# Low parts of every second output projection tile built by an accumulating DMA, and the last head's products put into score banks

## The chip, the cores and the metric

The kernel runs on one core of a Trainium2 chip (trn2). The metric is the device time in microseconds (us) of one execution. The core's engines run side by side, each through its own list of instructions in order: TensorE (PE, matrix products, with its weight loads as a row of their own, PEld), VectorE (DVE), ScalarE (ACT) and GpSimd (POOL). SyncE (SP) issues nearly all transfers, which sixteen DMA engines carry out.

## The reference

Two layers (`DEPTH = 2`) of a hybrid decoder trunk over 512 tokens, with 16 learned meta tokens put in front (`T = 528` columns in all), width 1024, all in float32. Each layer runs a causal pooling mixer and a latent attention with 8 heads beside each other on the same normalised input:

```python
h = RMSNorm(x)
[u_pool | z_pool | c_q | c_kv | k_rope | z_mla | g_pool | g_mla] = h @ W_in
y_pool = W_pool_up( PoolMix(u_pool) * silu(z_pool) )
y_mla  = W_mla_up( MLA(c_q, c_kv, k_rope) * silu(z_mla) )
x = x + W_out( sigmoid(g_pool) * y_pool + sigmoid(g_mla) * y_mla )
```

`MLA` normalises the latent query and key/value rows, expands them to 8 heads of 64 + 32 elements (the 32 with a rotary position), normalises queries and keys per head, and takes a causal softmax over the keys. The meta positions are dropped from the output.

## The kernel before

**Precision by splitting.** A float32 product is made of three products of a faster type (`fp32r`). A weight chunk `raw` of 128 rows by up to 512 columns is fetched by an SP DMA (`raw<-win`, `raw<-wout`, ...). `wload` then makes the high part `whi` with a Copy on ACT (L179) and the low part `wlo = raw - whi` with a subtraction on DVE (L180). Activations are split in the same way (L275, L276). `mm3` multiplies `whi·xh`, `whi·xl` and `wlo·xh` (L184, L185, L186) into the same PSUM accumulator.

**Staging.** `raw`, `whi` and `wlo` have three buffers each. Tiles marked `spare` (the odd `mu` tiles, L1005) take the pool `th`/`tl` instead. `stream()` is one generator over all weight tiles of both layers, in the order of `plan`: it loads up to four chunks ahead, and a tile of width 1024 (`D`) has two chunks of 512 columns. So a chunk of 512 columns feeds four 128x128 weight blocks, and each block is used in three products over every column segment: two segments of 264 columns in layer 0, one of 512 columns in layer 1 (the last tile of layer 1: two of 256).

**Order.** `Layer.go` writes the rest by hand: norms, pooling, attention heads and meta tokens are emitted at points of the stream, with `fill_now(ns)`, `fill(...)`, `up(name)` and `after(ns, fn)` letting so much of the stream pass between them. The order of each engine's instructions is then fixed once, when the kernel is built, by a scheduler that models time (`schedule_with_timeline_sim=True`). At run time each engine goes through its list and waits on semaphores.

**The places that the change touches.**

- `norm_sums` (L370): the row sums for the first norm, the products of ones with squares (L389), a short Newton chain on DVE for the inverse roots (`newton`), a write to DRAM (`ndr<-ny`, L420), and a read back spread over all partitions (`rinv<-ndr`, L426). In layer 0, `tables()` makes the rotary sine and cosine (DVE L293 to L303, ACT L300 and L301) between the write and the read.
- `pv` (L823): the product of a head's probabilities with its values. The probabilities are transposed into an `mm` bank, split into `th`, `tl` on ACT and DVE, and multiplied into the bank `o` (L845, L846). Odd heads also put four products for the meta tokens into a bank `tr` (L849 to L852), which ACT copies out (`racc`, L854).
- PSUM: `mmt()` gives one of four `mm` banks, `sct()` one of three score banks `S`, which are free once the last head's scores have been used; `o` is one bank.
- `meta_queries` (L877): in layer 0, the attention of the 16 meta queries from all heads' scores, called when the last head's first products and 2600 ns of stream have been emitted. Its second half comes `2 * LAG` later, and `meta_out` (L907) fills the 16 meta columns of `ogs`, which the first `mu` tile reads.
- `mu{m}` (L1004) and `o{m}` (L1008): eight tiles each per layer, at its end. `o{m}` is the output projection: 16 chunks of `wout` per layer, evicted by `ev_o` with a DVE instruction (L942).

Of the kernel before, what the change touches and what calls it, by code (L numbers as in the profile page):

```python
# [18 lines left out]
P = 128  # L19
# [52 lines left out]
def trunk(ctx, tc, xT, xrow, mrow, pos, win, wkr, wqb, wkb, wvb, wgr, wpu, wmu, wout, gains, const, yT):  # L72
# [17 lines left out]
    def slot(tag, dt=F32, bufs=1, w=W):  # L90
        return sl.tile([P, w], dt, tag=tag, name=nm(tag), bufs=bufs)
# [69 lines left out]
    class Gemm:  # L161
        def __init__(self, name, src, width, evac=None, xs=None, segs=None, body=None, gain=None):
            self.name, self.src, self.width, self.alloc = name, src, width, mmt
            self.evac, self.xs, self.segs, self.body, self.gain = evac, xs, segs, body, gain
            self.spare = False

    loads = [0]

    def wload(src, n, gain, spare):
        raw = early.pop(0) if early else fetch(src, n, rawt(), sp)  # L170
        loads[0] += 1
        pool, th, tl, nb = (tp, "th", "tl", 2) if loads[0] <= 2 or spare else (wp, "whi", "wlo", 3)
        if gain is not None:
            v = raw[:, :n].rearrange("p (k m) -> p k m", k=8)
            gp.tensor_mul(v, v, gain.unsqueeze(2).to_broadcast([P, 8, n // 8]))
            return raw, None
        hi = pool.tile([P, W if pool is tp else 512], F32R, tag=th, name=nm("whi"), bufs=nb)
        lo = pool.tile([P, W if pool is tp else 512], F32R, tag=tl, name=nm("wlo"), bufs=nb)
        act.activation(hi[:, :n], raw[:, :n], AF.Copy)  # L179
        dve.tensor_sub(lo[:, :n], raw[:, :n], hi[:, :n].bitcast(F32))  # L180
        return hi, lo

    def mm3(out, wh, wl, xh, xl, start, stop):
# [8 lines left out]
    def stream():  # L192
        flat = [(g_, c) for g_ in plan for c in range(0, g_.width, 512)]
        flat[1], flat[2] = flat[2], flat[1]

        def load(i):
            g_, c = flat[i]
            n = min(512, g_.width - c)
            return wload(g_.src[:, c:c + n], n, g_.gain, g_.spare)

        ahead = []
        for i in range(4):
            ahead.append(load(i))
            yield 0.0
        for i, (g_, c) in enumerate(flat):
            w = ahead.pop(0)
            if i >= 3 and i + 1 < len(flat):
                ahead.append(load(i + 1))
            final = c + 512 >= g_.width
            if g_.body is not None:  # L210
                yield from g_.body(c // 512, w)
            else:
                xs = g_.xs()
                K = len(xs)
                if c == 0:
                    g_.pss = [g_.alloc() for _ in g_.segs]
                k0 = c // P
                for ps, (a, b) in zip(g_.pss, g_.segs):
                    n = b - a
                    for k in range(k0, min(K, k0 + 4)):  # L220
                        o = (k - k0) * P
                        mm3(ps[:, :n], w[0][:, o:o + P], w[1][:, o:o + P],
                            xs[k][0][:, a:b], xs[k][1][:, a:b], k == 0, k == K - 1)
                        if k < K - 1 and (k - k0) % 2 == 1:
                            yield 6 * (n / 2.4)
                    if final:
                        g_.evac(ps[:, :n], a, b)
                        if b == g_.segs[-1][1]:
                            done.add(g_.name)
                        yield 6 * (n / 2.4)  # L230
            if final:
                done.add(g_.name)
# [80 lines left out]
    class Layer:  # L313
# [56 lines left out]
        def norm_sums(self):  # L370
            if self.l:
                fill_now(2600)
            else:
                rows = self.row_sums()
                for _ in range(8):
                    step()
                while (0, "ckv1") not in done:
                    next(rows)
                for _ in range(4):
                    next(rows)  # L380
            px, pc = mmt() if self.l else None, mmt()
            xs = self.xsq[::4] if self.l else []
            runs = [(px, t, m, m < 2, m >= len(xs) - 2) for m, t in enumerate(xs)]
            runs += [(pc, t, m, True, True) for m, t in enumerate(self.csq)]
            for k in range(0, len(runs), 2):
                for s, (a, b) in enumerate(FULL):
                    for ps, t, m, start, stop in runs[k:k + 2]:
                        g = 64 * s + 32 * (m % 2)
                        mm = pe.matmul(ps[g:g + 32, :HALF], ones[:, 0:32], t[:, a:b], start=start, stop=stop,  # L389
                                       tile_position=(0, g))  # L390
                        if t is not self.csq[1]:
                            behind(mm, self.csq_last)
            sums = tmp()
            for s, (a, b) in enumerate(FULL):
                if self.l:
                    act.activation(sums[0:64, a:b], px[64 * s:64 * s + 64, :HALF], AF.Copy)
                dve.tensor_copy(sums[64:128, a:b], pc[64 * s:64 * s + 64, :HALF])
            raw, norms = nsr[self.l], ndr[self.l]
            if self.l:
                sp.dma_start(raw, sums[0:97:32, 0:T])  # L400
            else:
                sp.dma_start(raw[2:4], sums[64:97:32, 0:T])
                for _ in rows:
                    pass
            C = T // 16
            parts = lambda d: d.rearrange("i (s c) -> s i c", c=C)
            fill_now(2600)
            nq = sm.tile([16, 4, C], F32, tag="nq", name=nm("nq"))
            na, nt, ny = (sm.tile([16, n, C], F32, tag=t, name=nm(t)) for t, n in (("na2", 2), ("nt2", 2), ("ny2", 3)))
            sp.dma_start(nq, parts(raw))  # L410
            dve.tensor_scalar(na[:, 0, :], nq[:, 0, :], 1.0 / D, EPS, op0=ALU.mult, op1=ALU.add)
            dve.scalar_tensor_tensor(out=na[:, 0, :], in0=nq[:, 1, :], scalar=1.0 / D, in1=na[:, 0, :],
                                     op0=ALU.mult, op1=ALU.add)
            dve.tensor_scalar(na[:, 1, :], na[:, 0, :], EPS, None, op0=ALU.mult)
            dve.tensor_scalar(ny[:, 2, :], na[:, 1, :], EPS, None, op0=ALU.mult)
            for m in range(2):
                dve.scalar_tensor_tensor(out=na[:, 1, :], in0=nq[:, 2 + m, :], scalar=1.0 / 256,
                                         in1=na[:, 1, :], op0=ALU.mult, op1=ALU.add)
            newton(ny[:, 0:2, :], na, nt)
            sp.dma_start(parts(norms), ny)  # L420
            self.inv, self.cinv = slot("rinv"), slot("q1")
            if self.l == 0:
                tables()
            fill_now(RET)
            for i, d in enumerate((self.inv, self.cinv)):
                behind(sp.dma_start(d[:, 0:T], norms[i:i + 1, :].partition_broadcast(P)), newest[0])  # L426
            self.st = [sct(), sct()]
# [395 lines left out]
        def pv(self, prev, js):  # L823
# [2 lines left out]
            h, pt, pm = prev  # L826
            p, odd = h // 2, h % 2
            if js[0] == 0:
                self.o = pp.tile([P, 512], F32, tag="o", name=nm("o"), bufs=1)
            ops = self.o  # L830
            if odd == 1 and js[0] == 0:
                self.pmr = sm.tile([P, 4, 3, 32], F32R, tag="pmr", name=nm("pmr"))
# [13 lines left out]
                pe.matmul(out, vt[:, j, h, :], tl[:, :n], start=False, stop=j == 3)  # L846
            if js[-1] != 3:
                if odd == 1:
                    tr = mmt()  # L849
                    for i in range(4):  # L850
                        pe.matmul(tr[0:96, P * i:P * (i + 1)], self.pmr[:, i].rearrange("p a b -> p (a b)"), identr,
                                  start=True, stop=True)  # L852
                    self.mt = slot("racc", F32R)
                    act.activation(self.mt[0:96, 0:512], tr[0:96, :], AF.Copy)  # L854
                return
# [97 lines left out]
        def register(self, nxt):  # L953
# [52 lines left out]
            for m in range(8):  # L1006
                add(f"mu{m}", wmu[l, m], 512, evac=self.ev_mu(m), xs=lambda: self.ogs, segs=XS)
                plan[-1].spare = m % 2 == 1  # L1008
            mg = lambda: self.mg
            for m in range(8):  # L1010
                add(f"o{m}", wout[l, m], D, evac=self.ev_o(m, nxt), xs=mg,
                    segs=[(NM, NM + SEQ // 2), (NM + SEQ // 2, T)] if self.last and m == 7 else XS)

        def gap(self):
            fill(FILL[self.l], (self.l, RESERVE[self.l]))

        def go(self, nxt):
# [44 lines left out]
                self.gap()  # L1062
            fill_now(1300)
            self.pv(prev, (0, 1))
            fill_now(2600)
            if not self.last:
                self.meta_queries()
            self.pv(prev, (2, 3))
            up("gm7")
            flush()  # L1070
# [85 lines left out]
```

## Time and profile before

| | |
|---|---|
| median of 3 runs | 784.38 us (784.22 to 784.66) |
| profiled execution | 784.25 us |
| its span in the profile | 782.5 us |
| granted TensorE clock | 1.00 in all slices |
| share of the span busy | PE 99%, DVE 69%, ACT 53%, POOL 26% |
| weight chunks split on DVE (L180) | 251 |
| DMA queue that SP issues to | 82.86 of 84.04 MB |

Some 1.8 us of the profiled execution lie outside the span. An instruction row of the timeline gives its start, its length, the engine, the line, the operation, output and inputs, the shape, a count, and in brackets the idle time before it that something ended. A row of the waits gives the waiting group, the releaser, the total, the count and the longest. The two output projections of this execution lie at about 340 to 402 us (layer 0) and 728 to 780 us (layer 1).

### The profile page before, as it was taken

To read this page: it belongs to the slowest core of one execution; us is meant where nothing else is said; L and a number is where in the kernel's file an instruction comes from. 1 tells how busy PE (TensorE), PEld (TensorE's weight loads), DVE (VectorE), ACT (ScalarE), POOL (GpSimd) and SP (SyncE) were. 2 spreads that over 40 slices of the span, in tenths; PEclk is the share of its full clock that TensorE was granted. 3 is DMA by queue.
4 is the path that set the end of the run, shared out by engine and by line. 5 is a ranking of instruction groups with operands and counts; after the bars stand their busy time and mean duration, and the time that the engine had idled before them with its cause. 6 is when DMAs were issued, how large, how long until landed. Compare 5 with 4: busy or idle time off the path is not lost.

```text
span 782.5 us, 14500 instructions
## 1 busy us (share of the span) xinstructions
PE 776.2 (99%) x5235; PEld 705.7 (90%) x5235; DVE 538.0 (69%) x1163; ACT 411.5 (53%) x938; POOL 206.8 (26%) x265
## 2 busy tenths in 40 slices
PE   9999999999999999999999999999999999999998
PEld 9999899999999999999998898887788888887887
DVE  6588787357779977675365587774477888665932
ACT  6755656545656565533354356455446666554421
POOL 1035504012343242052120335130132333410500
PEclk9999999999999999999999999999999999999999
DMA  8533233333323212324643323324242332222372
GB/s 297 153 104 95 77 124 104 108 96 102 92 74 92 79 63 74 95 81 143 182 137 97 103 82 96 125 88 142 72 124 89 95 89 80 66 78 68 101 231 99
DMA packets 54931, 84.04 MB, mean 107 GB/s; under 512 B 10006, under 2 KB 18582, under 8 KB 54860
## 3 DMA queue, kind: packets, MB, share of 16 engines
q1 hardware_dynamic: 54716, 82.86, 34.8%
q8 instruction: 41, 0.67, 0.4%
q14 instruction: 30, 0.25, 0.1%
q10 hardware_dynamic: 144, 0.26, 0.1%
HBM read 76.68 MB, written 4.29 MB: 103 GB/s over the span
## 4 chain that ended last, share of the span: by engine, by line
PE 94%; DVE 3%; DMA 1%; ACT 1%; issue 1%; POOL 0%; SPq 0%; ACTq 0%; DVEq 0%; POOLq 0%
PE mm L184 28%; PE mm L185 27%; PE mm L186 27%; PE mm L840 2%; PE S L184 2%; PE S L185 1%; PE S L186 1%; PE o L846 1%; PE o L845 1%; PE S L495 1%; DMA rinv<-ndr 1%; PE mm L454 0%; DVE wlo L180 0%; DMA xb<-xT 0%; DMA raw<-wmu 0%
## 5 line engine op out<-in xcount | busy, mean ns | idle before, releaser
L184 PE MATMUL mm<-hh,whi 128*128 128x264 f32 (+2 forms) x1096 | 346.3, 318 | 0.4 <-DVE u L538 0.2
L185 PE MATMUL mm<-hl,whi 128*128 128x264 f32 (+2 forms) x1096 | 343.6, 315 | 0.0
L186 PE MATMUL mm<-hh,wlo 128*128 128x264 f32 (+2 forms) x1096 | 342.6, 315 | 0.0
L180 DVE TENSOR_TENSOR wlo<-raw,whi 128x512 fp32r<-128x512 f32 (+2 forms) x251 | 188.9, 756 | 109.4 <-ACT whi L179 105.6
L179 ACT ACTIVATE whi<-raw 128x512 fp32r<-128x512 f32 (+2 forms) x251 | 150.3, 602 | 178.3 <-PE mm L185 130.0
L184 PEld LDWEIGHTS mm<-hh,whi 128*128 128x128 f32 x1096 | 205.7, 188 | 14.1 <-issue 1.3
L185 PEld LDWEIGHTS mm<-hl,whi 128*128 128x128 f32 x1096 | 206.3, 188 | 11.9
L186 PEld LDWEIGHTS mm<-hh,wlo 128*128 128x128 f32 x1096 | 205.4, 188 | 12.1
L743 POOL TENSOR_TENSOR tmp<-kp,bc 64x528 f32<-64x528 f32 x16 | 24.0, 1499 | 105.5 <-issue 90.1
L818 POOL TENSOR_TENSOR pm<-pa,rs 128x16 f32<-128x16 f32 x32 | 11.6, 362 | 150.0 <-DVE rs L813 150.0
L602 POOL TENSOR_TENSOR racc<-racc,tmp 128x264 f32<-128x264 f32 (+1 forms) x15 | 16.4, 1094 | 119.5 <-ACT tmp L601 94.3
L928 POOL TENSOR_TENSOR tmp<-tmp,xb 128x264 f32<-128x264 f32 (+1 forms) x24 | 27.1, 1152 | 58.7 <-DVE tmp L926 33.0
L774 DVE CUSTOM_DVE_ANT_0 S<-S,maskw,nqs 128x272 f32<-128x272 f32 (+4 forms) x80 | 38.4, 498 | 2.3 <-PE S L186 2.0
L781 ACT ACTIVATE cq<-S,bia 128x400 f32<-128x400 f32 (+2 forms) x48 | 24.6, 516 | 21.9 <-DVE bia L808 12.2
L184 PE MATMUL mm<-u,whi 128*128 128x264 f32 (+1 forms) x108 | 35.3, 327 | 0.0
L186 PE MATMUL mm<-u,wlo 128*128 128x264 f32 (+1 forms) x108 | 34.7, 322 | 0.0
L184 PE MATMUL mm<-cq,whi 128*128 128x264 f32 (+1 forms) x108 | 34.7, 321 | 0.0
L185 PE MATMUL mm<-cq,whi 128*128 128x264 f32 (+1 forms) x108 | 34.5, 321 | 0.0
L186 PE MATMUL mm<-cq,wlo 128*128 128x264 f32 (+1 forms) x108 | 34.5, 321 | 0.0
L276 DVE TENSOR_TENSOR tl<-mm,th 128x512 fp32r<-128x512 f32 (+1 forms) x64 | 29.3, 481 | 6.1 <-ACT th L275 5.1
L820 POOL TENSOR_TENSOR cq<-cq,rs 128x384 f32<-128x384 f32 (+1 forms) x32 | 32.3, 1009 | 0.0
L184 PE MATMUL mm<-q,whi 128*128 128x264 f32 (+1 forms) x96 | 29.9, 323 | 1.0 <-ACT q L275 0.7
(254 smaller groups left out, 1369.2 us busy)
## 6 DMA issues: line engine op xcount, KB each, us to landing
raw<-win SPq DMA_DIRECT2D x143, 256.0 KB, 2.6
raw<-wout SPq DMA_DIRECT2D x32, 256.0 KB, 2.9
bc<-kdr SPq DMA_DIRECT2D x16, 264.0 KB, 3.3
raw<-wpu SPq DMA_DIRECT2D x16, 256.0 KB, 2.7
raw<-wmu SPq DMA_DIRECT2D x16, 256.0 KB, 2.7
raw<-wqb SPq DMA_DIRECT2D x12, 256.0 KB, 2.7
xb<-xT SPq DMA_DIRECT2D x8, 264.0 KB, 5.2
tmp<-xT SPq DMA_DIRECT2D x16, 132.0 KB, 2.8
```

The lines of the kernel that those rows point to most:

```text
L179: act.activation(hi[:, :n], raw[:, :n], AF.Copy)
L180: dve.tensor_sub(lo[:, :n], raw[:, :n], hi[:, :n].bitcast(F32))
L184: pe.matmul(out, wh, xh, start=start, stop=False)
L185: pe.matmul(out, wh, xl, start=False, stop=False)
L186: newest[0] = pe.matmul(out, wl, xh, start=False, stop=stop)
L276: dve.tensor_sub(lo[:, a:b], src, hi[:, a:b].bitcast(F32))
L602: self.acc_last = gp.tensor_add(self.acc[:, a:b], self.acc[:, a:b], t[:, :b - a])
L743: gp.tensor_mul(kf[r0:r0 + 64, :], self.kp[r0:r0 + 64, :], bc[r0:r0 + 64, :])]
L774: dve.tensor_tensor_reduce(out=sv, in0=sv, in1=mask, scale=nqs[:, i, h:h + 1], scalar=3e38, op0=ALU.add, op1=ALU.min, accum_out=bia[:, c:c ...
L781: act.activation(pv, sv, AF.Exp, scale=-1.0, bias=bia[:, i:i + 1], accum_out=rs[:, c:c + 1])
L820: gp.tensor_mul(pt[i][:, NM:], pt[i][:, NM:], rs[:, i:i + 1].to_broadcast([P, n - NM]))
L928: gp.tensor_add(t[:, :b - a], t[:, :b - a], self.am[m][:, a:b])
```

## The change

Six edits are made together:

1. **Odd `o` tiles.** `o1`, `o3`, `o5`, `o7` of both layers (16 of the 32 `wout` chunks) are marked `added`. For these, ACT writes `whi` as before, then ACT writes `wlo = -raw` rounded to fp32r (a second Copy with scale -1.0; its rounding is that of `whi`, negated), and a DMA issued by GpSimd fetches the same chunk of `wout` again and adds it into `wlo`. The DVE subtraction falls away for them.
2. **`norm_sums`, layer 0.** Six calls of `next(rows)` instead of four before the products of ones with squares.
3. **`norm_sums`, both layers.** The `fill_now(RET)` behind the write of the norms is cut in two halves, and `tables()` (layer 0) comes between them.
4. **Last head of each layer.** The bank `o` and, as the head is odd, the bank `tr` of the meta products are taken from the score banks.
5. **`mu2` of layer 0** takes its bank from the score banks.
6. **`meta_queries`** is called ahead of the `fill_now(2600)` that preceded it. In layer 1 only the `fill_now` is there, as before.

```diff
     def wload(src, n, gain, spare, added):
...
         act.activation(hi[:, :n], raw[:, :n], AF.Copy)
-        dve.tensor_sub(lo[:, :n], raw[:, :n], hi[:, :n].bitcast(F32))
+        if added:
+            act.activation(lo[:, :n], raw[:, :n], AF.Copy, scale=-1.0)
+            gp.dma_start(out=lo[:, :n], in_=src, accum_op=ALU.add)
+        else:
+            dve.tensor_sub(lo[:, :n], raw[:, :n], hi[:, :n].bitcast(F32))
...
-                for _ in range(4):
+                for _ in range(6):
                     next(rows)
...
+            fill_now(RET / 2)
             if self.l == 0:
                 tables()
-            fill_now(RET)
+            fill_now(RET / 2)
...
             if js[0] == 0:
-                self.o = pp.tile([P, 512], F32, tag="o", name=nm("o"), bufs=1)
+                self.o = sct() if h == H - 1 else pp.tile([P, 512], F32, tag="o", name=nm("o"), bufs=1)
...
                 if odd == 1:
-                    tr = mmt()
+                    tr = sct() if h == H - 1 else mmt()
...
                 add(f"mu{m}", wmu[l, m], 512, evac=self.ev_mu(m), xs=lambda: self.ogs, segs=XS)
                 plan[-1].spare = m % 2 == 1
+                if (l, m) == (0, 2):
+                    plan[-1].alloc = sct
...
                     segs=[(NM, NM + SEQ // 2), (NM + SEQ // 2, T)] if self.last and m == 7 else XS)
+                plan[-1].added = m % 2 == 1
...
             self.pv(prev, (0, 1))
-            fill_now(2600)
             if not self.last:
                 self.meta_queries()
+            fill_now(2600)
             self.pv(prev, (2, 3))
```

More of the change, by code (lines that the diff above doesn't have):

```diff
@@ L164, in __init__, with wload @@
             self.evac, self.xs, self.segs, self.body, self.gain = evac, xs, segs, body, gain
-            self.spare = False
+            self.spare = self.added = False
     loads = [0]
-    def wload(src, n, gain, spare):
+    def wload(src, n, gain, spare, added):
         raw = early.pop(0) if early else fetch(src, n, rawt(), sp)
@@ L198, in load @@
             n = min(512, g_.width - c)
-            return wload(g_.src[:, c:c + n], n, g_.gain, g_.spare)
+            return wload(g_.src[:, c:c + n], n, g_.gain, g_.spare, g_.added)
         ahead = []
```

## The prediction

> **What bounds the kernel now.** I read the page's busy times and its chain first.
>
> ```profile
> PE 776.2 (99%) x5235; PEld 705.7 (90%) x5235; DVE 538.0 (69%) x1163; ACT 411.5 (53%) x938; POOL 206.8 (26%) x265
> PE 94%; DVE 3%; DMA 1%; ACT 1%; issue 1%; POOL 0%; SPq 0%; ACTq 0%; DVEq 0%; POOLq 0%
> ```
>
> PE is busy for 776.2 of 782.5 us, and the built order of the changed kernel holds as many matmuls as before. So the whole span can win only what PE now waits, and lose what PE is made to wait. The waits of PE (waiting group, releaser, total us, count, longest) say where:
>
> ```profile
> PE mm L184 <- ACT q L275: 0.7, 1, 0.7
> PE mm L184 <- DVE tmp L926: 0.3, 1, 0.3
> PE mm L389 <- ACT q L446: 0.2, 1, 0.2
> PE mm L184 <- DVE u L538: 0.2, 1, 0.2
> PE mm L184 <- ACT racc L854: 0.2, 1, 0.2
> ```
>
> Each is one short stop. The timeline of PE shows what three of them cost, if the start before the gap and the start after it are compared:
>
> ```profile
> 329.89 0.28 PE L186 MATMUL mm<-hh,wlo 128*128 128x264 f32 x1
> 330.88 0.51 PE L184 MATMUL mm<-q,whi 128*128 128x264 f32 x2 [0.71 <-ACT q L275]
> ...
> 336.69 0.28 PE L186 MATMUL mm<-q,wlo 128*128 128x264 f32 x1
> 337.25 0.39 PE L184 MATMUL mm<-q,whi 128*128 128x264 f32 x1 [0.28 <-DVE tmp L926]
> ...
> 703.97 0.39 PE L186 MATMUL mm<-hh,wlo 128*128 128x512 f32 x1
> 704.46 0.47 PE L845 MATMUL o<-th,vt 128*128 128x512 f32 x1
> 705.13 0.50 PE L184 MATMUL mm<-hh,whi 128*128 128x512 f32 x1 [0.20 <-ACT racc L854]
> ```
>
> The first is the first `mu` tile, waiting for the meta columns of `ogs`, last in the chain of `meta_queries`. The second is `mu2`, waiting for the bank that `mu0`'s eviction frees. The third pair is the last head of layer 1: its value product waits for `th`, and the next `gm` tile for the bank that `tr` holds until ACT has copied it. Edits 6, 5 and 4 aim at these three.
>
> The stretches of the output projections look different. In the windows (from:to; busy us and instructions of PE, PEld, DVE, ACT, POOL; granted clock, DMA share, GB/s), and in the group of the subtractions in the first of them:
>
> ```profile
> 340.00:402.00 62.00, 62.00 (x511) 62.00 (x510) 35.75 (x67) 24.90 (x46) 17.47 (x18) 1.00 0.51 150
> 728.00:780.00 52.00, 51.32 (x246) 42.48 (x244) 27.08 (x39) 13.24 (x22) 7.59 (x5) 1.00 0.48 154
> ...
> L180 DVE TENSOR_TENSOR wlo<-raw,whi 128x512 fp32r<-128x512 f32 x19 | 13.8, 728 | 14.6 <-ACT whi L179 14.4
> ```
>
> PE fills both, and DVE is busy for about half of either.
>
> **Edit 1, the subtractions that go.** 16 x 0.728 = 11.6 us of DVE work leave stretches in which PE never waits for DVE. Gain: 0. PE hides them now.
>
> **Edit 1, what comes.** 16 more Copies on ACT, 16 DMAs issued by POOL, and one new wait: the matmul L186 that reads `wlo` now waits for a landing. Nothing else on PE is affected, but everything behind that matmul is queued on PE in order. When must the DMA land? It can start only when the `wlo` buffer of three chunks ago is free and ACT has made its two passes. The ACT timeline gives the pace of PE, since a `whi` buffer comes free when the last of its products is done:
>
> ```profile
> 366.71 0.63 ACT L179 ACTIVATE whi<-raw 128x512 fp32r<-128x512 f32 x1 [2.30 <-PE mm L185]
> 372.56 0.63 ACT L179 ACTIVATE whi<-raw 128x512 fp32r<-128x512 f32 x1 [2.30 <-PE mm L185]
> ...
> 756.80 0.63 ACT L179 ACTIVATE whi<-raw 128x512 fp32r<-128x512 f32 x1 [2.14 <-PE mm L185]
> 762.35 0.63 ACT L179 ACTIVATE whi<-raw 128x512 fp32r<-128x512 f32 x1 [2.14 <-PE mm L185]
> ```
>
> In layer 0 a pair of these lies two chunks, 48 matmuls, apart: 5.85 / 48 = 0.122 us each. In layer 1 it is one chunk of 24: 5.55 / 24 = 0.231 us. Counted in the built order of the changed kernel, the matmuls between the one that frees the `wlo` buffer and the first that reads its new contents are, chunk by chunk: layer 0, 74, 53, 51, 53, 51, 62, 42, 52; layer 1, 39, 28, 24, 38, 24, 38, 26 (four of them half as wide), 40 (28 of them half as wide). Times the pace, less two passes of 0.63 us, the DMA has from issue to landing: layer 0, 7.8, 5.2, 5.0, 5.2, 5.0, 6.3, 3.9, 5.1 us; layer 1, 7.7, 5.2, 4.3, 7.5, 4.3, 7.5, 4.3, 4.7 us. So everything hangs on whether an accumulating landing takes less or more than some 4.3 us.
>
> The trace holds no POOL DMA and no accumulation. The nearest rows are the DMA issues of the same chunks by SP, in the first window and in the second (transfer, count, KB, median us from issue to landing):
>
> ```profile
> raw<-wout SPq DMA_DIRECT2D x15, 256.0 KB, 2.7
> ...
> raw<-wout SPq DMA_DIRECT2D x14, 256.0 KB, 3.7
> tmp<-scr SPq DMA_DIRECT2D x7, 256.0 KB, 3.3
> ```
>
> In layer 1 the same 256 KB take 1.0 us longer, beside other transfers of as many bytes. That is also how the new DMA will stand: the ACT pass that makes `-raw` frees `raw`, so SP's next fetch and POOL's accumulation start together, on DMA engines that are about half busy now and would carry half as many bytes again. Lower bound of a landing: 2.7 and 3.7 us, as if POOL's were SP's. Upper bound: twice that, 5.4 and 7.4 us, if the second operand, `wlo` itself, costs a second transfer in full. I take 1.3 us above SP's, 4.0 and 5.0 us: 1.0 for sharing, as between the two windows, and 0.3 for the issue, the length of an SP issue in the rows below. Layer 0 then is late once, by 0.14 us; layer 1 three times by 0.72 us (the eighth gains the stop of the seventh, whose window overlaps its own). A stop also lengthens the first matmul after it (row at 337.25: 0.39 us against 0.28), 0.11 each. Sum: 0.14 + 0.11 + 3 x 0.83 = **+2.7 us**. By the bounds it is 0 to about +16: at 5.4 and 7.4 us a second and a third chunk of each tile pair are late too.
>
> Beside the row, one rule. The Trainium skill ("DMA: Bandwidth & Descriptors", Anatomy of one DMA — SWDGE (gpsimd) path) fits a GpSimd DMA at 2.0 us plus bytes over 436 GB/s, which for 256 KB is an estimate of 2.6 us; by it no landing is late and this term is 0. The same page (Issuing engines are not separate DMA queues) speaks against the change: DMAs of all issuers interleave on the same 16 engines, so by it the sharing term of the sum stays. No row of this trace shows either for POOL.
>
> The 16 added Copies, 16 x 0.63 = 10 us on ACT, run in windows where ACT is busy for 24.90 of 62 and 13.24 of 52 us; later `whi` passes have slack behind them (2.30 and 2.14 us of idle time in the rows above). Cost 0; without that cover the same chunks would be late by up to 0.63 each. On POOL the issue stands ahead of the adds L928 and L347, and waits for ACT's pass; POOL is busy 17.47 of 62 us, and PE waits for neither add. Cost 0.
>
> **Edits 4, 5, 6: the three stops.** With each gone, PE goes on at its pace: 0.99 - 0.12 = 0.87; 0.56 - 0.12 = 0.44; (0.49 - 0.23) + (0.67 - 0.23) = 0.70. Together -2.0 us. Late next: the score banks are free once the last head's exponentials are done, which its products need anyway. `o` waiting for `th` (0.26) is not a bank's wait and may stay. I take **-1.75**; bounds -2.0 and -1.0.
>
> **Edits 2 and 3: the first norm.** The first 2510 matmuls keep their order, so edit 2 removes nothing from PE: the stop at L389 (0.2 us) waits for ACT's squares and stays. Edit 3 puts the tables behind the Newton chain. Rows of SP, the chain, ACT, DVE and PE around it:
>
> ```profile
> 42.25 1.28 ACT L300 ACT_TABLE_LOAD   x1
> 43.55 0.65 ACT L300 ACTIVATE tcos<-tmp 128x528 f32<-128x528 f32 x1
> 44.10 0.63 ACT L301 ACTIVATE tsin<-tmp 128x528 f32<-128x528 f32 x1
> ...
> 49.21 0.33 SPq L420 DMA_DIRECT2D ndr<-ny  x1
> 50.66 0.33 SPq L426 DMA_DIRECT2D rinv<-ndr  x1
> ...
> 50.66 4.00 DMA rinv<-ndr
> ...
> 54.75 0.43 DVE L538 TENSOR_TENSOR u<-mm,rinv 128x264 f32<-128x264 f32 x1 [0.62 <-DMA rinv<-ndr]
> ...
> 54.83 0.28 PE L186 MATMUL mm<-kh,wlo 128*128 128x264 f32 x1
> 55.33 0.36 PE L184 MATMUL mm<-hh,whi 128*128 128x264 f32 x1 [0.23 <-DVE u L538]
> ```
>
> The read back lands at 54.66, DVE evicts, PE has stopped for 0.50 - 0.12 = 0.38 us. Newton runs earlier without the tables between its steps, so this stop can go: -0.4. But the tables' 2.5 us of ACT and their DVE steps then stand in the next stretch, ahead of `whi` and `wlo` of the chunks that PE reads there; if 2.5 us exceed the slack of a chunk (2.30 above), the excess and as much again on DVE lie on PE: up to +1.5. Between them I take **+0.2**, nearer to the gain.
>
> **Sum.** -1.75 + 0.2 + 2.7 = +1.15. The profiled execution took 784.25, so 785.4; it lies 0.13 below the median, so **785.5 us**. What a measurement can tell from no change here is about 0.2%, 1.6 us.
>
> **The rivals.** *A, the landing is hidden (other side).* If an accumulation lands within 4.3 us in layer 1 and 3.9 in layer 0, no matmul waits, and -1.75 + 0.2 leaves 782.7 to 782.8, with all bounds together 782.0 to 784.9. For it: 2.7 and 3.7 us of SP's own fetches. Against it: in layer 1 only 0.6 us remain for the second operand and for sharing. The skill's fit, above, is on this side.
>
> *C, the DMA engines become the limit of the stage.* At 5.0 us in layer 0 and 6.0 in layer 1 the late chunks are: layer 0, 1.14 once and two at about 0; layer 1, 3 x 1.72 and 0.8 once; with restarts 7.75. Sum -1.55 + 7.75 = +6.2: **790.5 us**. It decides from about 5.2 us on, where the second chunk's cover goes as well. For it: shares of 0.51 and 0.48 that rise with every accumulation, and two operands for each. Against it: each accumulation has only one fetch beside it.
>
> *D, the tables late.* If A holds for the landings and the tables cost their +1.5, the gain shrinks to 0.25: 784.1.
>
> **How the numbers follow.** Forecast 0.38 (landings up to 1 us late; its own range 783.2 to 787.5), A 0.35, C 0.22, D 0.05. Faster by over 0.2% (below 782.8): three quarters of A and a little of the forecast, 0.28. Within: the rest of A, D, and some 0.45 of the forecast's range, 0.27. Slower: the rest, 0.45. The range takes A from 781.9 and C to 792.5, leaving out C's far end near the upper bounds and gains beyond the stops seen.
>
> **What would show it.** Right: no stops at the `mu` start and at the last head of layer 1; in the waits of PE a new row, L186 released by a POOL DMA, with three or four stops of about 0.7 us in layer 1's output projection and one or none in layer 0's; landings of 4.0 and 5.0 us among the DMA issues. A: no such row, landings under 4.3. C: six stops or more, raw fetches longer than 3.7 us. The forecast is wrong in kind if PE waits in the output projections for ACT's second pass or for `raw` instead, or if the time shows in the first 60 us.

## The result: 2.2% slower

The changed kernel took 803.12 us (median of 4 runs, 799.82 to 803.4), the kernel before 784.52 beside it: a ratio of 1.0221, 95% interval 1.0201 to 1.0242. The forecast was 785.5 us, with a range of 781.9 to 792.5; it was wrong by 17.6 us, on the side that it had called likeliest. The profiled execution took 802.99 us, its span is 801.1 us at a mean granted clock of 0.994.

In this kernel L188, L189 and L190 are the three products of `mm3`, L179 and L181 ACT's two Copies (`whi`, and `wlo = -raw`), L182 the GpSimd DMA, L279 and L280 the split of activations, L933 POOL's add in the eviction of a `mu` tile. Busy times and chain, from the page of the changed kernel:

```profile
PE 783.4 (98%) x5235; PEld 710.6 (89%) x5235; DVE 527.0 (66%) x1147; ACT 421.0 (53%) x954; POOL 219.0 (27%) x281
PE 86%; DMA 5%; issue 4%; DVE 2%; ACT 2%; POOL 1%; SPq 0%; POOLq 0%; ACTq 0%; DVEq 0%
```

DVE lost the 11 us of its 16 subtractions, and nobody gained by it. The chain, which held 94% of PE and 1% of DMA, now holds 5% of DMA. PE's own busy time has grown by 7 us with the same 5235 matmuls: some of them were slower. The waits of PE:

```profile
PE mm L190 <- DMA wlo<-wout: 11.4, 6, 4.7
...
PE mm L188 <- ACT hh L279: 1.0, 1, 1.0
```

The stops at the first `mu` tile, at `mu2` and at `racc` are gone, as edits 4 to 6 meant. In their place stand six waits for the accumulation's landing, and one (L279) for the split of the last `mu` tile. (A wait of 1.1 us by the warm-up products at the start, which every kernel here has, is left out here and below.) The DMA issues in the output projection of layer 0 (340 to 412 us), then of layer 1 (735 to 801 us):

```profile
raw<-wout SPq DMA_DIRECT2D x14, 256.0 KB, 3.4
wlo<-wout POOLq DMA_DIRECT2D x8, 256.0 KB, 5.5
...
raw<-wout SPq DMA_DIRECT2D x15, 256.0 KB, 4.3
wlo<-wout POOLq DMA_DIRECT2D x8, 256.0 KB, 5.3
```

A landing takes 5.5 and 5.3 us (single ones 4.1 to 6.6), and SP's fetches beside it have become 0.7 and 0.6 us longer. The timeline of PE at three of the stops:

```profile
358.20 0.28 PE L190 MATMUL mm<-hh,wlo 128*128 128x264 f32 x1
359.50 0.39 PE L188 MATMUL mm<-hh,whi 128*128 128x264 f32 x1 [1.02 <-ACT hh L279]
360.04 0.39 PE L189 MATMUL mm<-hl,whi 128*128 128x264 f32 x1 [0.15 <-DVE hl L280]
...
365.27 0.28 PE L188 MATMUL mm<-hh,whi 128*128 128x264 f32 x1
367.72 0.39 PE L190 MATMUL mm<-hh,wlo 128*128 128x264 f32 x1 [2.17 <-DMA wlo<-wout]
...
369.21 0.42 PE L188 MATMUL mm<-hh,whi 128*128 128x264 f32 x1
369.43 0.42 PE L189 MATMUL mm<-hl,whi 128*128 128x264 f32 x1
...
753.12 0.39 PE L189 MATMUL mm<-hl,whi 128*128 128x512 f32 x1
758.18 0.79 PE L190 MATMUL mm<-hh,wlo 128*128 128x512 f32 x1 [4.66 <-DMA wlo<-wout]
```

Beyond the pace, the stops come to 7.3 us in layer 0 (1.2, 0.4, 2.3, 0.3, 0.7 and 2.35, read off in this way) and 7.1 in layer 1 (4.8, 1.8 and two of 0.2). And after the long ones the matmuls stand 0.22 us apart instead of 0.12, and 0.43 instead of 0.23. The windows of 4 us name the cause in the column before the last two, the granted clock:

```profile
368.00:372.00 4.00, 4.00 (x24) 4.00 (x24) 0.87 (x2) 0.74 (x2) 0.00 (x0) 0.64 0.49 161
...
756.00:760.00 4.00, 1.82 (x4) 1.49 (x5) 0.00 (x0) 0.00 (x0) 0.00 (x0) 0.78 0.58 203
760.00:764.00 4.00, 4.00 (x15) 3.20 (x14) 0.69 (x1) 1.16 (x2) 0.25 (x1) 0.80 0.27 72
```

Over the span, (1 - 0.994) x 801.1 = 4.8 us of clock are missing, nearly all of it here. Stops and clock are 7.3 + 7.1 + 4.8 = 19.2 us; against the profiled execution without the accumulations (below, 782.72 us) the loss is 20.3.

### The profile page after: what moved, and what is told of

Read it like the earlier page. It is cut to its first block, busy times and chain, and to the rows that moved or that the text cites. A ratio compares the mean times of both kernels' runs of the same rounds, so it can differ in the third digit from the quotient of the medians.

```text
span 801.1 us, 14533 instructions
## 1 busy us (share of the span) xinstructions
PE 783.4 (98%) x5235; PEld 710.6 (89%) x5235; DVE 527.0 (66%) x1147; ACT 421.0 (53%) x954; POOL 219.0 (27%) x281
## 4 chain that ended last, share of the span: by engine, by line
PE 86%; DMA 5%; issue 4%; DVE 2%; ACT 2%; POOL 1%; SPq 0%; POOLq 0%; ACTq 0%; DVEq 0%
PE mm L188 25%; PE mm L190 25%; PE mm L189 24%; DMA wlo<-wout 5%; PE mm L845 2%; PE S L188 2%; PE S L189 2%; PE S L190 2%; PE o L851 1%; PE o L850 1%; PE S L500 1%; PE mm L459 0%; DMA xb<-xT 0%; ACT whi L179 0%; POOL cq L351 0%
## 5 line engine op out<-in xcount | busy, mean ns | idle before, releaser
L190 PE MATMUL mm<-hh,wlo 128*128 128x264 f32 (+2 forms) x1096 | 342.9, 317 | 11.5 <-DMA wlo<-wout 11.4
L188 PE MATMUL mm<-hh,whi 128*128 128x264 f32 (+2 forms) x1096 | 347.5, 319 | 1.4 <-ACT hh L279 1.0
L189 PE MATMUL mm<-hl,whi 128*128 128x264 f32 (+2 forms) x1096 | 345.0, 316 | 0.2 <-DVE hl L280 0.2
L179 ACT ACTIVATE whi<-raw 128x512 fp32r<-128x512 f32 (+2 forms) x251 | 150.6, 603 | 182.4 <-PE mm L189 133.9
L184 DVE TENSOR_TENSOR wlo<-raw,whi 128x512 fp32r<-128x512 f32 (+2 forms) x235 | 176.4, 754 | 98.1 <-ACT whi L179 93.1
L190 PEld LDWEIGHTS mm<-hh,wlo 128*128 128x128 f32 x1096 | 206.3, 190 | 26.2 <-DMA wlo<-wout 14.0
L188 PEld LDWEIGHTS mm<-hh,whi 128*128 128x128 f32 x1096 | 207.7, 190 | 14.7 <-issue 1.4
L189 PEld LDWEIGHTS mm<-hl,whi 128*128 128x128 f32 x1096 | 208.3, 190 | 12.5 <-DVE hl L280 0.4
L933 POOL TENSOR_TENSOR tmp<-tmp,xb 128x264 f32<-128x264 f32 (+1 forms) x24 | 26.5, 1136 | 55.6 <-DVE tmp L931 53.4
L188 PE MATMUL mm<-u,whi 128*128 128x264 f32 (+1 forms) x108 | 35.3, 327 | 0.0
L190 PE MATMUL mm<-u,wlo 128*128 128x264 f32 (+1 forms) x108 | 34.7, 321 | 0.0
L188 PE MATMUL mm<-cq,whi 128*128 128x264 f32 (+1 forms) x108 | 34.7, 321 | 0.0
L189 PE MATMUL mm<-cq,whi 128*128 128x264 f32 (+1 forms) x108 | 34.5, 321 | 0.0
L190 PE MATMUL mm<-cq,wlo 128*128 128x264 f32 (+1 forms) x108 | 34.5, 321 | 0.0
L182 POOL DMA_DIRECT2D wlo<-wout x16 | 14.5, 906 | 68.5 <-ACT wlo L181 66.5
L280 DVE TENSOR_TENSOR tl<-mm,th 128x512 fp32r<-128x512 f32 (+1 forms) x64 | 29.2, 482 | 6.2 <-ACT th L279 3.6
```

The lines of the kernel that those rows point to most:

```text
L188: pe.matmul(out, wh, xh, start=start, stop=False)
L189: pe.matmul(out, wh, xl, start=False, stop=False)
L190: newest[0] = pe.matmul(out, wl, xh, start=False, stop=stop)
L280: dve.tensor_sub(lo[:, a:b], src, hi[:, a:b].bitcast(F32))
L933: gp.tensor_add(t[:, :b - a], t[:, :b - a], self.am[m][:, a:b])
```

## The experiments

All times are medians; ratios are to the kernel before on the same chip, with 95% intervals. Two more kernels, which only measure something (the probe of landings and the inserted stops below), ran once each and are not in the table.

| kernel | us | ratio |
|---|---|---|
| changed | 803.12 | 1.0221 (1.0201 to 1.0242) |
| changed, no accumulations | 782.41 | 0.9963 (0.9949 to 0.9977) |
| before + edit 1 | 803.17 | 1.0234 (1.0216 to 1.0252) |
| changed, plain copy by POOL | 791.33 | 1.0083 (1.0067 to 1.0100) |
| changed, o1 without it | 790.83 | 1.0077 (1.0053 to 1.0101) |
| changed, four buffers | 783.09 | 0.9976 (0.9967 to 0.9985) |
| changed, a GpSimd DMA at the start | 797.58 | 1.0159 (1.0145 to 1.0174) |
| before + edits 4, 5, 6 | 782.56 | 0.9971 (0.9962 to 0.9980) |
| changed, no accumulations, tables back | 782.45 | 0.9971 (0.9960 to 0.9981) |
| before + edit 6 | 783.25 | 0.9978 (0.9969 to 0.9987) |
| before + edits 4, 5 | 783.59 | 0.9987 (0.9977 to 0.9996) |

**Which edit carries the loss.** First edit 1 taken out, then edit 1 alone on the kernel before:

```diff
-                plan[-1].added = m % 2 == 1
+                plan[-1].added = False
```

> The changed kernel without the accumulating DMAs: all weight chunks get their low parts on DVE again, edits 2 to 6 stay. Theory (the accumulations carry the whole loss; the two output projections went from -0.1 to +10.35 and from +8.86 to +18.6 us against before): what is left is +0.8 at the first norm, -1.1 at the mu start and -1.45 at the last head of layer 1, so about 782.7 us, and no stop of PE in the output projections. Rival (the bank and order edits move work into the output projections and share in the loss): over 786 us, with stops there.

> The kernel before with edit 1 alone. Theory: both output projections lose what they lost in the changed kernel, +10.4 and +9.7, so about 804 us. Rival (the loss needs the other edits, which shift the start of the stages against the transfers): under 795 us.

782.41 and 803.17 us: the theory held on both sides. By the ratios, edit 1 costs 20 us with the others in place and 18 without them. Without edit 1 the others together gain: the kernel without accumulations is the fastest form here together with the two that differ from it only at the first norm. Beside edit 1 their gain does not show; the ratios with and without them, 1.0221 and 1.0234, have intervals that overlap. The waits of PE without accumulations:

```profile
PE mm L188 <- DVE u L543: 0.6, 1, 0.6
PE mm L393 <- ACT q L451: 0.2, 1, 0.2
PE S L188 <- ACT hh L340: 0.2, 1, 0.2
```

All three lie in the first 60 us: behind the first norm PE does not stop any more. The stop at the first `u` eviction, which edit 3 was to take away, is still there. It scatters between executions: 0.6 us here, 0.4 in the changed kernel, none with four buffers (below); without edit 3, 0.2 in the kernel before and 1.1 in that with edit 1 alone.

**What makes the landing long.** The same DMA without its addition, in the same built order:

```diff
-            gp.dma_start(out=lo[:, :n], in_=src, accum_op=ALU.add)
+            gp.dma_start(out=lo[:, :n], in_=src)
```

> The changed kernel with the GpSimd DMA as a plain copy of the chunk into the low part, not an accumulation (so the low parts are not the differences); order and waits are the same. Theory a (the second operand makes the landing long): POOL's landings fall from a median of 5.4 us to the 4.2 of SP's fetches beside them, most stops go, about 790 us. Theory b (sharing of the 16 DMA engines and POOL's way of issuing make it long): landings stay at 5 us or more and the time at 800 us or more.

791.33 us, near the 790 of theory a. DMA issues of this run, layer 0 and layer 1:

```profile
raw<-wout SPq DMA_DIRECT2D x14, 256.0 KB, 2.5
wlo<-wout POOLq DMA_DIRECT2D x8, 256.0 KB, 4.5
...
raw<-wout SPq DMA_DIRECT2D x15, 256.0 KB, 3.4
wlo<-wout POOLq DMA_DIRECT2D x8, 256.0 KB, 3.3
```

The addition costs 1.0 us of landing in layer 0 and 2.0 in layer 1, and SP's fetches are shorter by 0.9 without it. But POOL's plain copy in layer 0 is still 2.0 us behind SP's: theory a is only part of it. The landing by itself was to be measured in the attention heads, on the kernel without accumulations:

```diff
+            n, acc = PROBE[self.l][h]
+            gp.dma_start(out=probe[0][:, 0:n], in_=wout[self.l, h][:, 0:n],
+                         accum_op=ALU.add if acc else ALU.bypass)
```

> The changed kernel without the accumulations in the output projections, and with one GpSimd DMA per head into a tile that nothing reads, in the attention heads, where the DMA engines are 25% to 32% busy: plain or accumulating, of 64, 128 or 256 KB, as a measurement of the landing by itself. Theory a (the accumulation itself is slow): an accumulating landing of 256 KB takes 1 us or more longer than a plain one of the same size even here, and the difference grows with the size. Theory b (sharing with the fetches makes it long): both land within 3.5 us here.

It missed its place: since nothing waits for these transfers, the scheduler put all 16 ahead, one after the other between 3.7 and 71.6 us. So each size and kind was measured a few times only, and beside the loads of the start (the run took 791.44 us). The eight landings of 256 KB, one DMA issue at a time: at 36.4 us plain, at 40.4 and 44.6 accumulating, at 49.1 plain, at 3.7 plain, at 10.6 accumulating, at 67.3 accumulating and at 71.6 plain:

```profile
probe<-wout POOLq DMA_DIRECT2D x1, 256.0 KB, 3.5
...
probe<-wout POOLq DMA_DIRECT2D x1, 256.0 KB, 3.9
...
probe<-wout POOLq DMA_DIRECT2D x1, 256.0 KB, 4.1
...
probe<-wout POOLq DMA_DIRECT2D x1, 256.0 KB, 2.8
...
probe<-wout POOLq DMA_DIRECT2D x1, 256.0 KB, 6.6
...
probe<-wout POOLq DMA_DIRECT2D x1, 256.0 KB, 6.8
...
probe<-wout POOLq DMA_DIRECT2D x1, 256.0 KB, 3.9
...
probe<-wout POOLq DMA_DIRECT2D x1, 256.0 KB, 4.9
```

The first four ran while the DMA engines were 54% to 64% busy: there the accumulating ones took 0.4 to 1.3 us longer. The next two ran at 95% and more, in the first loads: 6.6 and 6.8, plain or not. The last two go the other way, accumulating 3.9 at 47% and plain 4.9 at 64%. So busier DMA engines lengthen both kinds, and single landings scatter by as much as the addition costs; the surer figure for the addition is the 1.0 and 2.0 us of the output projections, with eight landings on each side. Pairs of 64 KB (plain 2.9 and 2.2, accumulating 4.8 and 3.5) differ at least as much as those of 256 KB, so the addition's part does not grow with the size, against theory a. Both theories named a part of the landing; how it splits for a single transfer stays open.

**Where in the output projection.** The accumulation left out of `o1` (`m % 2 == 1 and m > 1`):

> The changed kernel with the accumulation in o3, o5 and o7 only, not in o1. Theory (the largest stops come from the o1 chunks: their second Copy on ACT stands behind the splits of the last mu tiles, which wait for POOL, and POOL's own adds stand behind its DMA issue): the stops of 1.2 + 0.4 + 2.3 us in layer 0 and 4.8 us in layer 1 go, with the lower clock after the two long ones (some 1.4 and 1.8 us); about 791 us. Rival (the landing alone decides, and the stops come to whichever tile is first): 799 us or more.

790.83 us: two chunks of eight per layer carry 12 of the 20 us. Why these two? In layer 1 the rows of ACT, from the changed kernel, before the stop at 753:

```profile
748.25 0.63 ACT L279 ACTIVATE hh<-tmp 128x512 fp32r<-128x512 f32 x1 [0.63 <-POOL tmp L933]
...
749.97 0.63 ACT L279 ACTIVATE hh<-tmp 128x512 fp32r<-128x512 f32 x1 [0.56 <-POOL tmp L933]
750.51 0.62 ACT L181 ACTIVATE wlo<-raw 128x512 fp32r<-128x512 f32 x1
```

ACT's Copies stand in its list behind the splits of the last `mu` tiles, and those wait for POOL's adds. The DMA is issued at 751.5, lands 6.6 us later, and PE wants it at 753.35: 1.8 us of cover where the forecast had counted 5.2. In layer 0 it is POOL's list, in the changed kernel (ACT's pass, then POOL):

```profile
354.81 0.62 ACT L181 ACTIVATE wlo<-raw 128x512 fp32r<-128x512 f32 x1
...
354.41 0.75 POOL L933 TENSOR_TENSOR tmp<-tmp,xb 128x264 f32<-128x264 f32 x1
357.21 1.01 POOL L182 DMA_DIRECT2D wlo<-wout  x1 [2.05 <-DVE tmp L931]
357.95 1.04 POOL L933 TENSOR_TENSOR tmp<-tmp,xb 128x264 f32<-128x264 f32 x1
```

ACT's pass for this chunk had ended at 355.43, but the issue is recorded 1.8 us later, and the add behind it, for which the split of `mu7` and then PE wait, starts at 357.95: that is the stop of 1.2 + 0.4 us at 358, which no transfer caused. Since all later issues come 0.3 us after their pass, the next run put one small GpSimd DMA at the start of the program:

```diff
+    gp.dma_start(out=sl.tile([P, W], F32, tag="q3", name=nm("q3"), bufs=1)[:, 0:128], in_=const[:, 0:128])
```

> The changed kernel with one small GpSimd DMA (64 KB, into a tile that is overwritten later) at its start. In the changed kernel POOL's first accumulation is recorded 1.8 us after ACT's pass ended, all later ones 0.3 us after. Theory (a cost of the first GpSimd DMA of a program): here the first one of the output projection comes 0.3 us after the pass, the stops of 1.2 and 0.4 us before it go, about 801.5 us. Rival (it waits for something else at that place): the same 1.8 us, about 803 us.

The issue comes at 354.92, 0.3 us after its pass (354.00 + 0.62), and the stop at `o0` is gone. The pass and the issue in that kernel, ACT and then POOL (all lines one further):

```profile
354.00 0.62 ACT L182 ACTIVATE wlo<-raw 128x512 fp32r<-128x512 f32 x1
```

```profile
354.92 0.89 POOL L183 DMA_DIRECT2D wlo<-wout  x1 [0.57 <-ACT hh L280]
```

The time fell by more than expected, to 797.58: the delay had also pushed the second chunk of `o1` late, whose stop shrank from 2.3 to 0.2 us, and without a long stop there the clock kept up; the first chunk now stops PE for 0.6. That comes to some 4.6 us. Most of the rest is a stop of 2.35 us near the end of layer 0, in whose place two of 1.2 and 1.3 us stand, with no slow matmuls behind them. Nothing shows that the delay has to do with this.

**The price of a stop.** Six stops put into the kernel without accumulations, where no accumulation is near, by a chain of Copies on ACT that starts after the newest matmul and on which the next tile's products wait:

```diff
+                    for _ in range(STOPS.get(g_.name, 0)):
+                        last = act.activation(pad, pad, AF.Copy)
+                        if hold[0] is None:
+                            behind(last, newest[0])
+                        hold[0] = last
```

> The changed kernel without the accumulations, and with six stops of PE put in on purpose in layer 1: the products of one tile wait for a chain of one to six Copies of 128x512 on ACT (0.6 us each) that starts after the last matmul. Theory (the granted clock falls behind a stop of about 2 us or more, as behind the stops of 2.33, 2.35 and 4.82 us and not behind those of 1.81, 1.18 and 0.69): the matmuls behind the short stops go on at 0.231 us, those behind the stops of over 2 us run at about 0.43 us for some 3 us. Rival (the slow matmuls come from the DMA traffic or from the landing's own chunk): no slow matmuls here behind any stop.

The first matmul behind each, in the timeline (the bracket is the stop), and the windows behind them:

```profile
442.42 0.39 PE L194 MATMUL mm<-hh,whi 128*128 128x264 f32 x1 [1.41 <-ACT pad L229]
452.39 0.59 PE L194 MATMUL mm<-hh,whi 128*128 128x264 f32 x1 [2.38 <-ACT pad L229]
467.19 0.59 PE L194 MATMUL mm<-hh,whi 128*128 128x264 f32 x1 [3.73 <-ACT pad L229]
...
508.32 0.50 PE L194 MATMUL mm<-hh,whi 128*128 128x512 f32 x1 [2.99 <-ACT pad L229]
520.05 0.80 PE L194 MATMUL mm<-hh,whi 128*128 128x512 f32 x1 [5.22 <-ACT pad L229]
```

```profile
442.40:447.00 4.60, 4.58 (x37) 4.58 (x38) 0.93 (x2) 1.23 (x2) 1.87 (x2) 1.00 0.09 29
452.40:457.00 4.60, 4.60 (x26) 4.60 (x27) 0.69 (x1) 1.41 (x4) 0.00 (x0) 0.67 0.19 64
467.20:472.00 4.80, 4.80 (x22) 4.80 (x23) 3.36 (x10) 2.49 (x6) 3.20 (x5) 0.50 0.02 3
...
508.30:513.00 4.70, 4.68 (x20) 3.86 (x21) 2.40 (x8) 1.27 (x2) 0.00 (x0) 1.00 0.07 21
520.00:525.00 5.00, 4.95 (x14) 4.00 (x15) 0.00 (x0) 0.43 (x1) 0.00 (x0) 0.63 0.00 0
```

The clock falls to a half behind the stops of 2.38, 3.73 and 5.22 us (and behind the sixth, of 4.40), not behind 1.41, with the DMA engines nearly idle: the rival is out. But it didn't fall behind 2.99, so the length of a stop alone does not settle it. Other traces say the same: in the kernel without the accumulation in `o1`, half pace follows a stop of 1.91 us (753.5 to 755.4), but not one of 2.10 (396.6 to 398.7).

The ends of the slow stretches give a clue. In this run they lie at 455.4, 472.5, 486.2 and 523.8 us, so 17.1, 13.7 and 37.6 apart: 5, 4 and 11 times 3.42. Continue that grid of 3.42 us backwards. The stop of 2.38 (450.0 to 452.4) then has 2.0 us inside one step (448.6 to 452.0), while the stop of 2.99 (505.3 to 508.3) is cut at 506.7 into 1.4 and 1.6. In the changed kernel, counted back from the ends of their own slow stretches (372.4 and 410.0), the stops of 2.17 and 2.19 have 2.2 and 1.9 us inside one step; that of 1.65 has 1.2, counted on from 761.5. So what seems to decide is not the length, but how much of a stop falls inside one step: 1.9 us was enough, 1.6 was not. This is read off afterwards; no run was made to test it.

The run took 810.99 us: 28.6 more than without the stops, of which the waits themselves are 20.1; 0.015 x 809.2 = 12 us of clock are missing, some of it within the stops, where it costs nothing.

**Enough cover.** Four buffers of `whi` and `wlo` instead of three (with the small tile `mo` moved into the place of `smeta`, to make room):

```diff
-        ... else (wp, "whi", "wlo", 3)
+        ... else (wp, "whi", "wlo", 4)
```

> The changed kernel with four buffers of the high and low parts instead of three. In its built order 74 matmuls lie between a buffer's release and the wait in layer 0 (before 42 to 62 after the first), and 36 to 60 in layer 1 (before 24 to 40): 7.8 us and 7.0 us or more for the landing. Theory (the loss is lateness of landings of 4 to 6.6 us against their cover, and the clock after the stops): nearly all of the 20 us goes, no stop over 0.5 us in the output projections except the one in which POOL's first issue holds up its own add (1.6 us), 782.5 to 786 us. Rival (the DMA engines cannot carry the second read of the chunks in time, whenever it starts): landings grow, 795 us or more.

783.09 us. The waits of PE in that kernel (again without that of the warm-up products), and its DMA issues in the two stretches:

```profile
PE mm L873 <- ACT racc L859: 0.4, 1, 0.4
PE S L188 <- ACT hh L340: 0.4, 1, 0.4
```

```profile
wlo<-wout POOLq DMA_DIRECT2D x8, 256.0 KB, 5.1
...
wlo<-wout POOLq DMA_DIRECT2D x8, 256.0 KB, 4.4
```

The landings are 5.1 and 4.4 us against 5.5 and 5.3, still longer than the cover of the tightest chunks with three buffers (3.9 and 4.3), and no matmul waits for one. The stop of 1.6 us that had been expected to remain did not come: POOL issues its first accumulation here at 348.4 us, straight behind an add, and nothing waits. So lateness was the loss, of the landings and at `o0` of a split, with the clock behind it; the DMA engines can carry the second reading of the chunks (their share is 0.69 and 0.68 in the two output projections). It also shows what the removed subtractions are worth once nothing else stands in the way: ratios of 0.9976 against 0.9963 without accumulations, intervals that overlap; no gain that can be measured.

**The small edits.** Edits 4 to 6 alone; the tables back at their old place; edit 6 alone; edits 4 and 5 alone:

> The kernel before with edits 4, 5 and 6 alone (without the accumulations and without the two edits at the first norm). Theory (the first norm's two edits cost nothing that can be told from the scatter of the first 55 us, which was 0 to 0.7 us between kernels that are the same up to there): as the kernel without accumulations, 782.4 us within 0.5. Rival (they cost the forecast's 0.2 to 1.5 us, since the tables stand in front of the next chunks): 781.0 to 781.9.

> The changed kernel without the accumulations and with the tables back at their old place (edit 3 undone; edit 2 kept). Theory: 782.4 us within 0.5, as the run with edits 4 to 6 alone. Rival (the tables' 2.5 us on ACT ahead of the next chunks cost up to 1.5): 781.0 to 781.9 here, and the stop at the eviction of the first u tile as before, 0.2 us.

> The kernel before with edit 6 alone (the meta queries ahead of the 2600 ns of stream). Theory: the stop at the first mu tile of layer 0 (0.87 us) goes, the others stay: 783.5 to 783.8 us. Rival (the chain of the meta queries is bound by something else and ends as late): no change, 784.5.

> The kernel before with edits 4 and 5 alone (banks). Theory: the stop at mu2 (0.44 us) and the pair at the last head of layer 1 (0.70 us) go, that at the first mu tile stays: 783.2 to 783.5 us. Rival (the wait of the last head's value product for its probabilities, 0.26 us, stays, and mu2 waits for the eviction work anyway): 784.0 or more.

782.56 and 782.45 us against 782.41 with all of edits 2 to 6: the first norm's edits cost and gain nothing that can be measured. Edit 6 alone gave 783.25, a little more than expected: its trace has neither the stop at the first `mu` tile nor the one at `mu2`. Edits 4 and 5 alone gave 783.59, near the 783.2 to 783.5 expected, but in part by other gains than those counted on. The pair at the last head of layer 1 went, 0.8 us. The wait at the first `mu` tile fell from 0.7 to 0.3 us. And the stop at `mu2` moved three tiles on, to `mu5`, with its old length. The wait at the first `mu` tile, and the row at `mu5`:

```profile
PE mm L188 <- ACT q L279: 0.3, 1, 0.3
...
345.78 0.36 PE L188 MATMUL mm<-q,whi 128*128 128x264 f32 x1 [0.28 <-DVE tmp L930]
```

(In that kernel `mu0` starts at 330.6 and a tile takes 2.93 us, so this is `mu5`.) So edit 5 did take the stop away from `mu2`, but by itself it only put it off. With the earlier meta queries the stop is gone from both places.

## Why the prediction was wrong

- **Right: what bounds the kernel, and that the subtractions gain nothing.** With the landings covered, the kernel without the 16 subtractions is no faster.
- **Right: the three stops.** Forecast -1.75 us with bounds of -2.0 and -1.0. Edits 4 to 6 alone have a ratio of 0.9971, 2.3 us (1.6 to 3.0). In kind one reason was off: a bank for `mu2` alone did not save its 0.44 us, it moved the stop to `mu5`; edit 6 is what removed it.
- **The first norm: forecast +0.2, measured 0.** Neither the -0.4 nor the +1.5 between which it was taken can be told: the stop at the first `u` eviction is 0.4 us in the changed kernel and 0.2 before, and none or 1.1 in others. The profiles of kernels that are built alike up to there differ by up to 0.7 us in the first 24 us, more than the whole term.
- **Wrong: "Sum: 0.14 + 0.11 + 3 x 0.83 = +2.7 us".** It measured 20. The mechanism, a matmul that waits for the landing and all of PE behind it, is what happened; three sizes in it failed.
  1. *The landing*, taken as 4.0 and 5.0 us, was 5.5 and 5.3. Put into the same sum, with the same cover, these give about 2.9 + 3.1 us of lateness and 8 restarts of 0.11, some 7 us instead of 2.7. It is about rival C's landing, and C's marks came (six stops, fetches over 3.7 us in layer 1), but its 790.5 us were 12.6 too few, for the other two reasons.
  2. *The cover*: "It can start only when the `wlo` buffer of three chunks ago is free and ACT has made its two passes." The count then took ACT to make them at once. In `o1` ACT's list put the splits of the `mu` tiles in front, and the issue came when 1.8 of 5.2 us were left. On POOL, "PE waits for neither add. Cost 0." was wrong too: the issue stood in front of the add of `mu7`, on which the split and then PE wait. Leaving `o1` out of edit 1 took 12 us off; with the delay of the first issue gone the time was 5.5 lower, some 4.6 of it in `o0` and `o1`, so largely inside the same 12.
  3. *The price of a stop*: "A stop also lengthens the first matmul after it ... 0.11 each." Behind most stops of about 2 us and more it is 3 us and more at half the clock, 4.8 us of clock here. The trace of before had no stop of over 1.1 us, so it could not show this.
- **The Trainium skill beside it.** By its fit (DMA: Bandwidth & Descriptors, Anatomy of one DMA — SWDGE (gpsimd) path) 256 KB from GpSimd would land in an estimated 2.6 us. The nearest runs are the plain copies at about half-busy engines, 2.8 and 3.5 us (4.9 at 64%); the accumulations, 5.5 and 5.3 beside the fetches, are far from it. The trace agrees with the other rule, that DMAs of all issuers interleave on the same 16 engines (the Trainium skill, same page, Issuing engines are not separate DMA queues): SP's fetches grew by 0.6 to 0.7 us with POOL's beside them, and a plain GpSimd copy took 6.6 us at full engines against 2.8 to 3.5 at half-busy ones. The Trainium skill (TensorE: Matmul & The Clock Gate, What's actually happening) has TensorE's clock fall to a half after an idle window of some 3.4 us that runs freely. The halving agrees, and so does the grid of 3.42 us in the run with stops. That the window has to be idle as a whole does not: 1.9 us of a stop inside one step were enough. That page was not weighed in the prediction. With stops of 0.7 us as forecast it would have added nothing to the sum.

## What to carry to other kernels

A DMA that takes the place of an engine's instruction is priced by its landing under the load of its own stage and by its cover, and the cover is counted from the real place of the issue in the lists of the engines before it: ask what stands in front of the instruction that starts it, and what stands behind its issue. Where PE is otherwise never idle, an operand that is late by some 2 us can cost more than its lateness, since the clock may fall too. A shorter DMA (the plain copy) took away 12 us here, one more buffer 20. And where the engine that is relieved is not waited for, the best outcome is nothing: here it needed a fourth buffer to come back to that.

## What was not expected of the hardware

- Behind seven of the eight stops of 2.17 us and more (idle time in brackets) in the changed kernel and in the run with stops, matmuls ran at half their pace for some 3 to 5 us (0.22 against 0.12 us apart, 0.43 against 0.23); behind one, of 2.99 us, they did not. Behind the two stops of 2.17 and 2.19 us this began only some 1.4 us after the stop. The slow stretches end on a grid of 3.42 us, as worked out above.
- The first GpSimd DMA of the program was recorded 1.8 us after the pass that it waited for, with POOL idle; with another GpSimd DMA far ahead of it, 0.3 us. Where POOL had been idle for 9.7 us before (the kernel without the accumulation in `o1`) the first came after 0.3 us as well. So being the first is not enough for the delay. The cause is not shown.
- An accumulating DMA of 256 KB from GpSimd took 1.0 and 2.0 us longer than a plain one in the two output projections. Alone, the difference ranged from 1.3 us longer to 1.0 us shorter, with few samples, and at full DMA engines both took about as long, 6.8 against 6.6 us.
